# First layer's mixer: TensorE's order fixed step by step from the gates on, and one gate or output projection ahead of the first chunk

## The chip, the cores and the metric

The kernel runs on one core of one Trainium2 chip. The metric is the device time of one execution in microseconds (us). Before the change it is 2372.28 us, the median of 3 runs (2371.1 to 2372.58).

## What is computed

The reference is a trunk of two decoder layers on one sequence of 1024 tokens with 1024 features. The first layer mixes tokens with an mLSTM, a matrix memory that is carried from one chunk of 128 tokens to the next; the second uses latent attention over keys and values that are made once from the first layer's output. Each mixer is followed by an MLP. All inputs and outputs are fp32. The change concerns the first layer's mixer alone:

```python
proj = h @ w_in                               # h: normed and modulated input, 1024 x 1024
q, k, v, ig, fg, og = jnp.split(proj, ...)    # 8 heads: q, k of 64, v of 128, one input and one forget gate each
# per head and chunk of 128 tokens, with b = cumsum(log_sigmoid(f)) and m a running maximum:
log_d = b[t] - b[s] + i[s]    (s <= t)
w_intra = exp(log_d - m[t]);  w_inter = exp(b + m_prev - m[t])
num = w_inter * (q @ C) + ((q @ k.T) * w_intra) @ v
C = decay * C + (w * k).T @ v                 # state for the next chunk
h = num / max(|den|, exp(-m))
out = (rmsnorm(h) * sigmoid(og)) @ w_out
```

The product of q and k with its weights is called a score below, `og` the output gate, and the last line's product the output projection.

## The kernel before, in words

**Products.** Every fp32 matrix product is made of three TensorE products of operands split into a high and a low part (`mm3`, lines 230 to 234). A 128-row weight panel is loaded by SyncE into a `raw` buffer (4 of them) and split by `wsplit` (lines 186 to 193): ScalarE rounds it into `wh` (line 189), VectorE takes the rest into `wl` (line 190). `wh` and `wl` come from a pool of 8, so four panels are held at a time. One panel of a projection to feature-major layout feeds 24 products of 128x128 by 128x512; a panel of v does so too.

**Halves.** The 1024 tokens are treated as two halves of 512, `hfs[0]` and `hfs[1]`. For each half the mixer's work is cut into generators; each `yield` ends a step:

- `qk_in` projects q and k, 8 projections of 24 products each. For the first half this is done earlier, by `qk_pairs`.
- `gates_in` (line 662) makes 16 products for the gates (lines 678, 679), then `gates0` (line 738): a chain of small operations on 8 partitions, each dependent on the one before, almost all on VectorE (lines 743 to 787) with five on ScalarE (lines 752, 754, 775, 777, 779). Its second step transposes three results on TensorE (line 792, 12 small matmuls into one `pc` tile) and copies them (line 794). Line 779 makes the last of those three inputs.
- `v_in` (line 693) projects v token-major: 2 column halves of 4 weight panels, 24 products per panel, two steps per panel, into `pm` tiles.
- `intra0` (line 797) makes the scores for four pairs of heads: for each head a broadcast matmul into a `pc` tile (line 808) and four Exp on ScalarE (line 812); then the scores of two heads into two `ps` tiles, 64 rows each (line 820); VectorE multiplies (line 825); a last matmul (line 833) and lines 834 and 835 scale q and keep the decay. The two heads of a pair use different rows of TensorE's array (`ts(r, 64)`) and are issued alternately in the code.
- `chunks0` (line 852) goes through the four chunks of the half, three steps each: numerators (lines 869 and 876) and transposes of k (line 883, then VectorE line 885); the state's update (line 918); normalising and transposing the result (line 933).
- `og0` (line 726) is the gate projection with its three ScalarE passes (lines 731 to 733), `wout` the output projection, `split_o` (line 839) gates the chunk results and splits them for that projection (lines 845, 848, 849).

`ps`, `pc` and `pm` are PSUM pools of two tiles each. Two background generators, `bg0` and `bg1` (`bgs` for both in a row), make the adaLN vectors of later stages. A step multiplies a loaded panel on VectorE (lines 358, 360) and ends in four transposes on TensorE (line 340) and a sum (line 342); they fill gaps.

**What sets the order.** The code is written in one order, but a list scheduler at build time with its own estimate of durations reorders instructions per engine by readiness and priority. `tc.issue_after(i)` ties what is issued within it to come behind instruction `i`. Each engine executes its own list strictly in that order, waiting on semaphores where inputs or buffers are not ready. Before the change only the chunk stages (`in_turn`, line 1937) are tied: every step's TensorE work is placed behind the last TensorE instruction of the step before. In the first half `weave` mixes one step of v with 1.5 steps of scores and one of the background; in the second `weave_n` takes the rest of the q, k and v steps with 0.8 of scores each. In both, the scheduler decides what stands where.

## Time and profile before

| | |
|---|---|
| median of 3 runs | 2372.28 us |
| the profiled execution | 2374.59 us, of which 2372.9 us are the span of its instructions |
| mean granted TensorE clock | 0.995 |
| busy: TensorE (PE) | 2331.0 us (98%) |
| busy: VectorE (DVE) | 1605.9 us (68%) |
| busy: ScalarE (ACT) | 1098.1 us (46%) |
| first gate product of the first half | 81.30 us |
| first product of the first half's chunks | 149.03 us |
| first gate product of the second half | 221.12 us |
| first product of the second half's chunks | 333.75 us |

The span is counted from the first instruction to the last. A row of the timeline gives the start, the duration, engine, source line, the operation, output tile and inputs, and, in brackets, how long the engine was idle before it and which instruction's end released it. Matmuls overlap: the duration of one is longer than the distance to the next, so that distances of starts tell what each costs. An fp32 matmul (lines 792 and 820) is recorded twice, so that four of them read x8. SyncE is SP, GpSimd is POOL. Stretches of the span can be asked for with each engine's busy time and the granted clock (PEclk) in them.

### The profile page before, as it was taken

To read this page: it belongs to the slowest core of one execution; us is meant where nothing else is said; L and a number is where in the kernel's file an instruction comes from. 1 tells how busy PE (TensorE), PEld (TensorE's weight loads), DVE (VectorE), ACT (ScalarE), POOL (GpSimd) and SP (SyncE) were. 2 spreads that over 40 slices of the span, in tenths; PEclk is the share of its full clock that TensorE was granted. 3 is DMA by queue.
4 is the path that set the end of the run, shared out by engine and by line. 5 is a ranking of instruction groups with operands and counts; after the bars stand their busy time and mean duration, and the time that the engine had idled before them with its cause. 6 is when DMAs were issued, how large, how long until landed. Compare 5 with 4: busy or idle time off the path is not lost.

```text
span 2372.9 us, 31774 instructions
## 1 busy us (share of the span) xinstructions
PE 2331.0 (98%) x11797; PEld 1947.3 (82%) x11797; DVE 1605.9 (68%) x2649; ACT 1098.1 (46%) x1818; POOL 156.2 (7%) x353
## 2 busy tenths in 40 slices
PE   7999999999999999999999999999999999999998
PEld 5778778888888788888888888888888888989997
DVE  6567866877575677877773967766666478457556
ACT  4355334654343354444444544534444445655543
POOL 1000000000001110111110120001001000000000
PEclk9999999999999999999999999999999999999999
DMA  9353564545566876677753666885544552657562
GB/s 313 125 155 95 167 194 137 169 134 158 166 191 175 247 231 200 178 213 206 211 163 111 200 198 197 255 285 161 179 129 132 146 168 86 188 176 218 165 183 89
DMA packets 404252, 420.72 MB, mean 177 GB/s; under 512 B 27428, under 2 KB 301921, under 8 KB 400513
## 3 DMA queue, kind: packets, MB, share of 16 engines
q1 hardware_dynamic: 398176, 385.02, 51.6%
q0 software_dynamic: 5920, 33.66, 6.3%
q8 instruction: 93, 1.52, 0.3%
q14 instruction: 63, 0.51, 0.1%
HBM read 359.37 MB, written 92.80 MB: 191 GB/s over the span
## 4 chain that ended last, share of the span: by engine, by line
PE 85%; DVE 6%; DMA 5%; ACT 2%; issue 2%; SPq 0%; DVEq 0%; ACTq 0%
PE ps L232 14%; PE ps L233 13%; PE ps L234 13%; PE pm L232 10%; PE pm L233 10%; PE pm L234 10%; PE pc L234 2%; PE pc L233 2%; PE pc L232 2%; DMA raw<-in_a_w_in_dram 2%; DVE wl L190 1%; PE pc L1676 1%; DMA raw<-in_mlp_w_dram 1%; DMA lw<-wl 1%; ACT wh L189 1%
## 5 line engine op out<-in xcount | busy, mean ns | idle before, releaser
L190 DVE TENSOR_TENSOR wl<-raw,wh 128x1024 fp32r<-128x1024 f32 (+2 forms) x382 | 458.9, 1203 | 378.7 <-ACT wh L189 277.5
L189 ACT CAST wh<-raw 128x1024 fp32r<-128x1024 f32 (+2 forms) x382 | 394.6, 1036 | 685.6 <-PE ps L232 234.0
L232 PE MATMUL ps<-k,wl 128*128 128x512 f32 (+1 forms) x1432 | 546.3, 381 | 0.3 <-DVE tmc L746 0.2
L234 PE MATMUL ps<-k,wh 128*128 128x512 f32 (+1 forms) x1432 | 539.4, 377 | 0.0
L233 PE MATMUL ps<-k,wh 128*128 128x512 f32 (+1 forms) x1432 | 537.7, 376 | 0.0
L232 PEld LDWEIGHTS ps<-k,wl 128*128 128x128 f32 x1432 | 269.9, 189 | 52.4 <-issue 3.4
L234 PEld LDWEIGHTS ps<-k,wh 128*128 128x128 f32 x1432 | 269.6, 188 | 50.2 <-issue 0.7
L233 PEld LDWEIGHTS ps<-k,wh 128*128 128x128 f32 x1432 | 270.0, 189 | 48.9 <-issue 1.4
L198 DVE TENSOR_TENSOR k<-k,pm 128x512 f32<-128x512 f32 (+1 forms) x254 | 211.2, 859 | 84.9 <-PE pm L234 83.5
L232 PE MATMUL pm<-hd,wl 128*128 128x512 f32 x512 | 202.0, 394 | 0.5 <-ACT hd L508 0.5
L233 PE MATMUL pm<-hd,wh 128*128 128x512 f32 x512 | 200.1, 391 | 2.0 <-DVE hd L509 2.0
L234 PE MATMUL pm<-hd,wh 128*128 128x512 f32 x512 | 200.1, 391 | 0.0
L232 PE MATMUL pm<-wh,hd 128*128 128x512 f32 x488 | 192.1, 394 | 3.6 <-ACT raw L1568 3.4
L233 PE MATMUL pm<-wl,hd 128*128 128x512 f32 x488 | 190.4, 390 | 0.0
L234 PE MATMUL pm<-wh,hd 128*128 128x512 f32 x488 | 190.2, 390 | 0.0
L1568 ACT ACTIVATE raw<-pm,sm 128x128 f32<-128x128 f32 (+3 forms) x64 | 47.5, 742 | 151.8 <-DVE sm L1567 114.9
L509 DVE TENSOR_TENSOR hd<-tmp,hd 128x512 fp32r<-128x512 f32 x128 | 88.1, 689 | 40.5 <-ACT hd L508 39.9
L233 PEld LDWEIGHTS pm<-hd,wh 128*128 128x128 f32 x512 | 96.5, 188 | 22.9 <-DVE hd L509 2.8
L232 PEld LDWEIGHTS pm<-hd,wl 128*128 128x128 f32 x512 | 96.6, 189 | 21.0 <-ACT hd L508 0.9
L234 PEld LDWEIGHTS pm<-hd,wh 128*128 128x128 f32 x512 | 96.5, 189 | 20.3
L1024 POOL COPY sm<-sm 128x1 f32<-128x1 f32 x128 | 48.5, 384 | 978.9 <-DVE sm L1023 942.3
L232 PEld LDWEIGHTS pm<-wh,hd 128*128 128x128 f32 x488 | 91.7, 188 | 23.7 <-ACT raw L1568 5.5
(395 smaller groups left out, 4013.5 us busy)
## 6 DMA issues: line engine op xcount, KB each, us to landing
raw<-in_mlp_w_dram SPq DMA_DIRECT2D x240, 512.0 KB, 4.4
raw<-in_ada_w_dram SPq DMA_DIRECT2D x80, 512.0 KB, 4.4
raw<-in_a_w_in_dram SPq DMA_DIRECT2D x48, 512.0 KB, 4.5
sums<-in_mlp_w_dram POOLq DMA_DIRECT2D x96, 256.0 KB, 4.6
raw<-sums SPq DMA_DIRECT2D x64, 256.0 KB, 3.7
xs<-k SPq DMA_DIRECT2D x40, 256.0 KB, 3.6
raw<-in_kv_ada_w_dram SPq DMA_DIRECT2D x16, 512.0 KB, 4.0
raw<-in_a_w_out_dram SPq DMA_DIRECT2D x16, 512.0 KB, 4.7
```

The lines of the kernel that those rows point to most:

```text
L189: nc.scalar.copy(hi[:, :n], r[:, :n])
L190: i = nc.vector.tensor_sub(lo[:, :n], r[:, :n], hi[:, :n].bitcast(F32))
L198: return f(*a, **k)
L232: nc.tensor.matmul(o, ll, rh, start=start, stop=False, **m)
L233: nc.tensor.matmul(o, lh, rl, start=False, stop=False, **m)
L234: pe_last[0] = nc.tensor.matmul(o, lh, rh, start=False, stop=stop, **m)
L509: nc.vector.tensor_sub(lo, u, hi.bitcast(F32))
L1024: now = nc.gpsimd.tensor_copy(seen, flag)
L1568: nc.scalar.activation(pr[:, :n], f, AF.Exp, bias=m, scale=SCALE, accum_out=l)
L1676: nc.tensor.transpose(pt[:, ts(2 * e + i, P)], u.prs[i][:, ts(b + e, P)], ident)
```

## The change

`go`, which runs one step of a generator and ties its TensorE instructions behind those of the step before, moves up and is used for nearly everything from the first half's gates to the second half's chunks. `share` runs a main generator step by step and, by given rates, background and side steps between them. `some_of` gives the first n steps of a generator.

First half: the gate products; five steps of v, each with one background step; the gates' transposes; then each further v step is followed by one background step and on average 1.85 score steps, and what is left of the scores comes at the end. Second half: gate products, two q/k steps, `split_o`, two more q/k steps with two background steps each, the gates' transposes, then the remaining four q/k steps with 2 score steps and 3 background steps each, then the v steps with 0.9 and 1.7.

`in_turn` takes one step of the wide work (the gate projection in the first half, the output projection of the first half in the second) ahead of the first chunk step, and none behind that first step; its background work is tied too. 67 background steps are taken before the MLP in place of 71. The number and kind of instructions of each engine are unchanged.

```diff
--- before.py
+++ after.py
@@ -1934,34 +1934,56 @@
         ada_kv(0), ada_line(kv_cols()[2:] + ada_cols(1, SH1) + ada_cols(1, SC1))
     )
 
+    last, end = [None], object()
+
+    def go(gen):
+
+        traced = nc.cur_bb.bb.instructions
+        top = traced[-1]
+        if last[0] is None:
+            r = next(gen, end)
+        else:
+            with tc.issue_after(last[0]):
+                r = next(gen, end)
+        for i in reversed(traced):
+            if i is top:
+                break
+            if i.engine == pe_last[0].ins.engine:
+                last[0] = i
+                break
+        return r
+
     def in_turn(wide, steps, fill):
 
-        traced = nc.cur_bb.bb.instructions
-        last = [None]
-
-        def go(gen):
-            top = traced[-1]
-            if last[0] is None:
-                r = next(gen, StopIteration)
-            else:
-                with tc.issue_after(last[0]):
-                    r = next(gen, StopIteration)
-            for i in reversed(traced):
-                if i is top:
-                    break
-                if i.engine == pe_last[0].ins.engine:
-                    last[0] = i
-                    break
-            return r
-
+        go(wide)
         n = 0
-        while go(steps) is not StopIteration:
-
-            if n % 3 < 2:
+        while go(steps) is not end:
+
+            if n and n % 3 < 2:
                 go(wide)
-            next(fill, None)
+            go(fill)
             n += 1
-        drain(wide)
+        while go(wide) is not end:
+            pass
+
+    def share(main, side, bg, per, bgs_per):
+
+        a = b = 0.0
+        while go(main) is not end:
+            a, b = a + per, b + bgs_per
+            while b >= 1.0:
+                b -= 1.0
+                go(bg)
+            while a >= 1.0:
+                a -= 1.0
+                go(side)
+
+    def some_of(g, n):
+        for _ in range(n):
+            v = next(g, end)
+            if v is end:
+                return
+            yield v
 
     bgs = chain(bg0, bg1)
     drain(qk_pairs(hfs[0], w0, modulate0(hfs[0].h, xT0, 1)))
@@ -1969,23 +1991,32 @@
         nc.sync.dma_start(
             xt_d[0][2 * b * P : (2 * b + 2) * P].rearrange("(k p) n -> p k n", p=P), xT0.t[b]
         )
-    drain(with_bg(gates_in(hfs[0]), bgs, 1))
+    g0, v0 = gates_in(hfs[0]), v_in(hfs[0])
+    go(g0)
     x1 = load_x1()
-    drain(weave(with_bg(v_in(hfs[0]), bgs, 1), intra0(hfs[0]), 1.5))
+    share(some_of(v0, 5), iter(()), bgs, 0, 1.0)
+    go(g0)
+    scored = intra0(hfs[0])
+    share(v0, scored, bgs, 1.85, 1.0)
+    while go(scored) is not end:
+        pass
     y1 = rms_x1(x1)
     hfs[1].h = Split()
     n1 = norm0(hfs[1].h, x1, y1, A0, adac(0, SH1))
     in_turn(og0(hfs[0], hdv), chunks0(hfs[0]), n1)
     drain(n1)
 
-    drain(gates_in(hfs[1]))
-    main = chain(twice(qk_in(hfs[1])), v_in(hfs[1]))
-    for _ in range(4):
-        next(main)
+    g1, qk1, scored = gates_in(hfs[1]), qk_in(hfs[1]), intra0(hfs[1])
+    go(g1)
+    go(qk1)
+    go(qk1)
     drain(split_o(hfs[0]))
-    for _ in range(2):
-        next(main)
-    drain(weave_n(with_bg(main, bgs, 1.7), intra0(hfs[1]), 0.8))
+    share(some_of(qk1, 2), iter(()), bgs, 0, 2.0)
+    go(g1)
+    share(qk1, scored, bgs, 2.0, 3.0)
+    share(v_in(hfs[1]), scored, bgs, 0.9, 1.7)
+    while go(scored) is not end:
+        pass
     drain(bg0)
     B0 = gate(1, NG(0, 1), adac(0, G1))
     A1 = gain(2, NG(0, 2), adac(0, SC2))
...
-    last, end = [None], object()
-
-    def go(gen):
...
```

How the change moves instructions shows at three places. In these rows stands the source line, the operation, the output and the inputs with the program's numbers, and the shape; the lines are those of the kernel before.

First place: TensorE in the first half, around the gates' transposes (`tmc_111`, `tmc_115` and `tmc_112` are the three results of the gate chain, the last one from line 779; `pm` are v's accumulators, `wh` and `wl` v's weight panels, `k4` the input's parts). Before:

```order
L232 MATMUL pm_132_750<-wh_155_866,k4_53_293 128x512
L792 MATMUL pc_119_705<-ident_64,tmc_111_658 128x8
L233 MATMUL pm_132_750<-wl_156_867,k4_52_292 128x512
L234 MATMUL pm_132_750<-wh_155_866,k4_52_292 128x512
L232 MATMUL pm_131_749<-wh_164_923,k4_55_295 128x512
L233 MATMUL pm_131_749<-wl_165_924,k4_54_294 128x512
L234 MATMUL pm_131_749<-wh_164_923,k4_54_294 128x512
```

After:

```order
L232 MATMUL pm_126_722<-wh_140_803,k4_53_293 128x512
L233 MATMUL pm_126_722<-wl_141_804,k4_52_292 128x512
L234 MATMUL pm_126_722<-wh_140_803,k4_52_292 128x512
L792 MATMUL pc_142_819<-ident_64,tmc_111_658 128x8
L792 MATMUL pc_142_819<-ident_64,tmc_115_667 128x8
L792 MATMUL pc_142_819<-ident_64,tmc_112_659 128x8
```

Before, the first transpose stood among the products of v's third panel, the second 22 rows later inside the fourth, and the third right after three more products; 84 products of v lay between the gate products and the third one. After, all twelve stand together behind 60 products of v, in the middle of its third panel, and the next product of v stands behind them.

The chain itself, on VectorE, from the third operation on (`wl` are low parts of weight panels; `tmc` the chain's values). Before:

```order
L745 COPY tmc_112_659<-ps_110_641 8x512
L190 TENSOR_TENSOR wl_165_924<-raw_163_921,wh_164_923 128x1024
L746 COPY tmc_113_660<-ps_110_641 8x512
L747 SCALAR_TENSOR_TENSOR tmc_112_659<-tmc_113_660,cols_72,tmc_112_659 8x512
L751 SCALAR_TENSOR_TENSOR tmc_113_660<-tmc_112_659 8x512
L753 TENSOR_SCALAR tmc_114_666<-tmc_113_660 8x512
```

After:

```order
L753 TENSOR_SCALAR tmc_114_666<-tmc_113_660 8x512
L755 SCALAR_TENSOR_TENSOR tmc_113_660<-tmc_114_666,tmc_113_660 8x512
L190 TENSOR_TENSOR wl_162_929<-raw_160_926,wh_161_928 128x1024
L756 SCALAR_TENSOR_TENSOR tmc_115_667<-tmc_112_659,tmc_115_667 8x512
L757 TENSOR_TENSOR tmc_115_667<-tmc_115_667,tmc_113_660 8x512
L760 SCALAR_TENSOR_TENSOR tmc_112_659<-ones_69,tmc_115_667 8x128 x4
L763 TENSOR_TENSOR tmc_111_658<-tmc_111_658,tmc_112_659 8x512
```

Before, one panel's line 190 stood within the chain, early. After, one stands here and another some rows further on, between two of the scans of line 766: two in all. In the second half it is one before and two after; there the eight operations of line 845 (which `split_o` issues) stand ahead of the chain in both, and the four of line 849 inside it in both.

Second place: TensorE at the scores of the first half (`ps` take the scores, `pc` the broadcasts and the background's transposes). Before, from the second pair on (the first stands head by head among v's second and third panels):

```order
L340 MATMUL pc_147_842<-ident_64,tma_117_700 128x128 x4
L820 MATMUL ps_161_909<-k4_79_373,k4_81_375 128x128 x4
L833 MATMUL pc_149_851<-RM_124,selW_118 128x512
L808 MATMUL pc_153_858<-RM_124,e8_116 128x512
L820 MATMUL ps_162_910<-k4_79_373,k4_81_375 128x128 x4
L808 MATMUL pc_159_887<-RM_124,e8_116 128x512
L833 MATMUL pc_167_946<-RM_124,selW_118 128x512
L820 MATMUL ps_179_1003<-k4_80_374,k4_82_376 128x128 x4
L808 MATMUL pc_172_971<-RM_124,e8_116 128x512
```

After, at the first pair, from a product of v's fourth panel on:

```order
L234 MATMUL pm_126_722<-wh_148_856,k4_54_294 128x512
L340 MATMUL pc_150_874<-ident_64,tma_131_742 128x128 x4
L808 MATMUL pc_152_882<-RM_124,e8_116 128x512
L820 MATMUL ps_153_888<-k4_79_373,k4_81_375 128x128
L820 MATMUL ps_154_889<-k4_79_373,k4_81_375 128x128
```

Before, the four matmuls of one head stood together, and other kinds stood between the heads and the pairs. After, the two heads of a pair alternate (the last two rows here repeat three times more), and 24 or 36 products of v stand between one pair and the next. So it is with all four pairs of the first half. In the second half, pairs one and two stand head by head in both kernels; pair three alternates in both, and pair four alternated before with two interruptions and does so now with none.

Third place: TensorE in the first chunk of the first half (line 876 are the numerators, line 883 the transposes of k, line 580 and line 545 work for the second half's norm, line 918 the update of the state, `ps_247` the gate projection). Before, from the last product of that projection on:

```order
L234 MATMUL ps_247_1285<-k4_54_294,wh_245_1281 128x512
L580 MATMUL ps_250_1320<-ident_64,k4_122_727 128x128 x2
L580 MATMUL ps_250_1320<-ident_64,k4_123_728 128x128 x2
L876 MATMUL pm_227_1223<-k4_127_741,hd_169_968 128x130 x2
L876 MATMUL pm_227_1223<-k4_127_741,hd_187_1058 128x130
L876 MATMUL pm_227_1223<-v8_126_739,hd_187_1058 128x130
L545 MATMUL pc_249_1314<-ident_64,sm_216_1207 128x128 x4
L918 MATMUL pc_253_1332<-k4_127_741,tmc_229_1237 64x130 x4
```

After, from the last numerator on:

```order
L876 MATMUL pm_233_1253<-v8_121_712,hd_190_1100 128x130
L883 MATMUL pc_234_1262<-ident_64,k4_81_375 128x128 x2
L883 MATMUL pc_234_1262<-ident_64,k4_82_376 128x128 x2
L580 MATMUL ps_248_1312<-ident_64,k4_117_700 128x128
L545 MATMUL pc_247_1306<-ident_64,sm_214_1199 128x128 x4
L580 MATMUL ps_248_1312<-ident_64,k4_117_700 128x128
L580 MATMUL ps_248_1312<-ident_64,k4_118_701 128x128 x2
L918 MATMUL pc_251_1324<-k4_122_714,tmc_235_1267 64x130 x4
```

Before, the 24 products of the gate projection stood between line 883 and line 918. After, they stand ahead of the numerators, and between 883 and 918 there are only the transposes of lines 580 and 545. In the second half the output projection moves in the same way, and there line 918 follows line 883 directly.

More of the change, by code (lines that the diff above doesn't have):

```diff
@@ L2048, in some @@
         return v != "end"
-    last, end = [None], object()
-    def go(gen):
-        traced = nc.cur_bb.bb.instructions
-        top = traced[-1]
-        if last[0] is None:
-            r = next(gen, end)
-        else:
-            with tc.issue_after(last[0]):
-                r = next(gen, end)
-        for i in reversed(traced):
-            if i is top:
-                break
-            if i.engine == pe_last[0].ins.engine:
-                last[0] = i
-                break
-        return r
     def two_streams(dense, other, fill=iter(()), more=4):
```

## The prediction

> **What bounds the kernel.** The page comes first, and of it the chain of work that ended last.
>
> ```profile
> PE 85%; DVE 6%; DMA 5%; ACT 2%; issue 2%; SPq 0%; DVEq 0%; ACTq 0%
> ```
>
> TensorE is the bound. The change makes it do the same instructions in another order, so it can gain or lose only three things: time in which TensorE waits, time at a lower clock, and the small price of alternating between kinds of matmul. What TensorE waits for, from 68 to 150 us (the first half's gates, v and scores), as total, times and longest:
>
> ```profile
> PE pm L233 <- DVE wl L190: 1.3, 1, 1.3
> PE pm L876 <- DVE v L722: 1.2, 1, 1.2
> PE ps L820 <- DVE hd L825: 0.9, 2, 0.5
> PE pc L340 <- ACT tmc L812: 0.5, 1, 0.5
> ```
>
> And from 220 to 345 us, the second half's (two of 0.2 are left out):
>
> ```profile
> PE pm L869 <- DVE v L722: 2.3, 1, 2.3
> PE pc L340 <- ACT tmc L812: 1.0, 1, 1.0
> PE pm L233 <- DVE wl L190: 0.3, 1, 0.3
> ```
>
> A weight panel that comes late, scores that wait for their buffers, a chunk that waits for the last copy of v: 3.9 us and 3.6 us, so the most there is to win is small. TensorE's timeline says what surrounds them.
>
> ```profile
> 110.65 1.16 PE L820 MATMUL ps<-k,k 64*128 64x128 f32 x8
> 111.73 0.51 PE L833 MATMUL pc<-RM,selW 128*128 128x512 f32 x1
> ...
> 144.73 0.39 PE L234 MATMUL pm<-wh,k 128*128 128x512 f32 x1
> ...
> 147.45 0.39 PE L234 MATMUL pm<-wh,k 128*128 128x512 f32 x1
> 149.03 1.13 PE L876 MATMUL pm<-k,hd 128*128 128x130 f32 x8 [1.20 <-DVE v L722]
> ...
> 297.89 1.16 PE L820 MATMUL ps<-k,k 64*128 64x128 f32 x16
> 298.98 0.73 PE L232 MATMUL pm<-wh,k 128*128 128x512 f32 x2
> ```
>
> From 144.73 to 147.45 are twelve products of 128x512, 0.227 us each. To 149.03 it is 1.58, so that wait cost 1.35 us, 0.15 more than its 1.20; I add this to each. One head's four scores cost 1.08 us (110.65 to 111.73). Where the heads alternate, at 297.89, both cost 1.09: half. Last, the granted clock (the third number from the right) in stretches of 3.4 us:
>
> ```profile
> 121.60:125.00 3.40, 3.19 (x8) 2.52 (x9) 3.40 (x5) 0.66 (x1) 2.58 (x1) 0.50 0.84 273
> 824.80:828.20 3.40, 1.59 (x8) 1.00 (x7) 2.82 (x5) 1.50 (x2) 0.52 (x1) 1.00 0.98 270
> 828.20:831.60 3.40, 3.40 (x10) 2.62 (x9) 3.08 (x3) 0.50 (x1) 0.00 (x0) 0.50 1.16 430
> 329.80:333.20 3.40, 1.67 (x8) 1.05 (x6) 3.29 (x7) 0.68 (x1) 0.00 (x0) 1.00 0.82 219
> 333.20:336.60 3.40, 2.69 (x20) 2.16 (x21) 3.40 (x6) 1.96 (x4) 0.00 (x0) 1.00 0.74 213
> ```
>
> After a stretch with much idle time TensorE runs the next at half clock, which costs half of it, 1.7 us. The two slow stretches begin 706.6 us apart, 207 times 3.413. Read on that grid, 1.81 us of idle time (3.40 less 1.59, at 824.80) brought one and 1.73 (at 329.80) didn't. The one at 121.60 follows the 1.3 us for a panel, among the thin matmuls of the scores.
>
> **What the change removes.** In the first half the four kinds of wait go with the order that made them, the last because a projection now stands ahead of the chunk: 3.9 + 5 x 0.15 = 4.6 us. The slow stretch at 121.60 goes with them, 1.7. All four pairs alternate: 4 x 1.08 = 4.3. Together 10.6. In the second half 3.6 + 3 x 0.15 = 4.0 go, and the interruptions of one pair, of which no row is shown: 0.6, an estimate of about half of its 1.09. Together 4.6.
>
> **What it adds: the gates' transposes.** TensorE now reaches line 792 after a fixed number of products, whether the chain is done or not, and the rest of v or of q and k queues behind it.
>
> ```profile
> 85.12 0.69 DVE L743 COPY tmc<-ps 8x512 f32<-8x512 f32 x1 [4.49 <-PE ps L679]
> ...
> 87.22 1.20 DVE L190 TENSOR_TENSOR wl<-raw,wh 128x1024 fp32r<-128x1024 f32 x1
> ...
> 91.77 0.68 DVE L755 SCALAR_TENSOR_TENSOR tmc<-tmc,tmc 8x512 f32<-8x512 f32 x1
> ```
>
> ```profile
> 100.86 0.63 ACT L779 ACTIVATE tmc<-tmc 8x512 f32<-8x512 f32 x1 [0.31 <-DVE tmc L778]
> ...
> 248.71 0.61 ACT L779 ACTIVATE tmc<-tmc 8x512 f32<-8x512 f32 x1
> ```
>
> ```profile
> 225.35 0.39 PE L232 MATMUL ps<-k,wl 128*128 128x512 f32 x1
> ```
>
> First half: the chain is released by the gate products at 85.12 and its last value is there at 101.49, 16.4 us later, with one line 190 (1.20) inside. A second makes it 17.6. TensorE's cover is 60 products, 13.6 us: with the hand-overs of 0.1 it stands for 4.1 us. Before, the cover was 84 products and a pair of scores. Second half: TensorE goes on from the gates at 225.35, and the last value is there at 249.32, 24.0 us later; a second line 190 makes it 25.2; the cover is four projections, 96 x 0.227 = 21.8: 3.4 us.
>
> **The clock behind these waits.** Of 4.1 us at least 2.0 lie in one stretch of the 3.413 grid wherever it falls, so a slow stretch follows. Where that one overlaps the wait itself it costs less; I take 1.5. The 3.4 can be cut into 1.7 and 1.7, which by the row at 329.80 is let pass, so 0.9. The Trainium skill, "TensorE: Matmul & The Clock Gate", Part 1, has the clock fall after at least one idle window of about 3.4 us on a free-running grid, and the section "Why this matters for your kernels" warns of gaps over about 3 us only; by that the first wait would hold such a window at one position in five, the second hardly ever, and the sum below would be 2.1 us better. The trace agrees on the grid, but its clock fell after less than a whole idle window.
>
> **Buffers.** What is placed in TensorE's order by hand can stand before its buffer is free. Waits of this kind are the 0.5 and 1.0 at line 340 and the 0.9 at line 820; the upper end is a panel that is asked for late:
>
> ```profile
> raw<-in_a_w_in_dram SPq DMA_DIRECT2D x48, 512.0 KB, 4.5
> ```
>
> First half: a broadcast (line 808) whose `pc` tile is still to be read by line 834, which stands on VectorE behind a line 190 of such a panel. Between 0.5 and 4.5; I take 2.0, since a panel is asked for ahead by the buffers that it has. Second half: background transposes and scores at three places, 0.5 each, 1.5; between 0 and 3.
>
> **The chunk stages.** Before, line 918 waited once, although a projection stood ahead:
>
> ```profile
> 155.93 0.60 PE L580 MATMUL ps<-ident,k 128*128 128x128 f32 x4
> ...
> 157.26 1.05 PE L545 MATMUL pc<-ident,sm 128*128 128x128 f32 x8
> 158.25 0.66 PE L918 MATMUL pc<-k,tmc 128*64 128x130 f32 x8
> 159.41 0.55 PE L918 MATMUL pc<-k,tmc 128*64 128x130 f32 x5 [0.50 <-ACT tmp L548]
> 150.64 0.69 DVE L885 TENSOR_TENSOR tmc<-pc,gc 128x512 f32<-128x512 f32 x1 [0.29 <-PE pc L883]
> 155.67 1.05 ACT L189 CAST wh<-raw 128x1024 fp32r<-128x1024 f32 x1 [0.67 <-PE ps L232]
> ```
>
> That 0.5 goes. Now line 918 of the first chunk comes 1.6 us after line 883 (0.60 of line 580 and 0.99 of 545, from its start to the next), while line 885 may stand behind a line 190: 1.20 + 0.69 and 0.3 of hand-over, less 1.6, is 0.6. Line 580 behind the next projection needs a buffer that is freed behind a cast (1.05): 1.3, between 0.5 and 2. Fewer alternations in three chunks: 0.6 won, an estimate of 0.1 for each of six. Net 0.5 - 0.6 - 1.3 + 0.6, 0.8 lost. In the second half line 918 follows line 883 at once: 0.69 + 0.3 = 1.0 lost.
>
> **The sum.** First half 10.6 - 4.1 - 1.5 - 2.0 - 0.8 = 2.2 won. Second half 4.6 - 3.4 - 0.9 - 1.5 - 1.0 = 2.2 lost. Four background steps move behind the MLP's start: 16 transposes in a stage with waits of its own, nothing taken, 1 us either way. In all nothing, 2374.6 against the profiled 2374.59. That execution was 2.3 above the median of 2372.28, so the forecast is 2372.3: within 0.2% of before, 4.7 us, about what a measurement of this kernel can tell from no change.
>
> **Rivals.** Faster: the waits at line 792 are short. The two line 190 fall into gaps of the chain, the clock isn't lowered, and buffers are free in time. Then 2 x 1.2, 2.4 and 3.5, together 8.3 us, are won on the sum: 2364.0. For it: the waits that go stand in the trace, those that come are worked out by hand. Against: 60 products (13.6) are shorter than even the bare chain, 16.4 - 1.2 = 15.2. 0.30.
>
> Slower: a loop between the engines stretches the chain. The line 190 inside it works on a panel whose `wh` buffer is free only when v's first panel is used up on TensorE, and whose cast takes 1.05 us on ScalarE; VectorE would wait there with the chain queued behind it, and TensorE waits for the chain. In the first half v's first panel ends 24 x 0.227 = 5.4 us after the gate products, with cast and hand-overs 6.7, while VectorE gets there 91.77 + 0.68 - 85.12 - 1.20 = 6.1 after them. It decides from 0.5 us on; if casts queue too, it is 2 us in each half, and a wait of 6 us holds a second stretch that lowers the clock, another 1.7: 2378.0. For it: the margins are that thin. Against: in the second half panels are used up well ahead. 0.18.
>
> That the order isn't what the text says is excluded by its rows; that what goes and what comes cancel is the forecast, 0.52.
>
> **Range.** From the faster to the slower rival, 2364.0 to 2378.0; the bounds of the buffers (2.5 up, 1.5 down in the first half, 1.5 in the second) lie within. Over 0.2% faster 0.30, within 0.52, slower 0.18.
>
> **What would show it.** Right: a wait of about 4 and one of about 3.4 us at line 792, released by line 779, and a slow stretch behind the first; scores as x16 in 1.1 us in the first half; the first numerators near 151.5 us (149.03 less 3.0, and 24 products of the moved projection, 5.4); no wait over 2 us ahead of the second half's chunks. Wrong: no wait at line 792, or one of 6; new waits over 2 us at line 820 or 808; or a difference that arises behind 400 us.

## The result, and the profile after

The changed kernel takes 2386.23 us (median of 4 runs, 2384.61 to 2388.04) against 2371.77 us before on the same chip: a ratio of 1.0061, 95% interval 1.0044 to 1.0078, so 14.5 us slower. The forecast was 2372.3 with a range from 2364.0 to 2378.0. The profiled execution took 2386.92 us with a span of 2385.2.

TensorE is busy for no longer than before (2326.2 us, where it was 2331.0), and in the chain of work that ended last a part has moved from it to VectorE and the loads:

```profile
PE 2326.2 (98%) x11797; PEld 1944.6 (82%) x11797; DVE 1604.8 (67%) x2649; ACT 1095.6 (46%) x1818; POOL 156.2 (7%) x353
...
PE 82%; DVE 7%; DMA 7%; ACT 2%; issue 2%; SPq 0%; DVEq 0%; ACTq 0%
```

TensorE has 82% of the chain where it had 85%, DVE 7% instead of 6 and DMA 7% instead of 5.

To see where the time goes, the two traces are laid over each other at equal work: TensorE's matmuls are counted by their columns, and at each count the time of the changed kernel less that of before is taken. (Counted by starts or by ends of the matmuls, such a difference comes out up to 0.4 us otherwise.) At 80 us of before the difference is -0.1 us, at 222 us -3.9, at 365 us +6.4, at 890 us +13.4 and at 2356 us +12.3. So the first half of the mixer **won** 3.8 us, the second half **lost** 10.3, and 7.0 were lost between 365 and 890 us, where the code is the same and only the four background steps are still to be done.

The first half, as TensorE's waits between 68 and 160 us (total, times, longest):

```profile
PE pc L792 <- ACT tmc L777: 3.2, 1, 3.2
PE pc L808 <- ACT tmc L812: 2.3, 1, 2.3
PE pc L792 <- ACT tmc L779: 0.7, 1, 0.7
PE pc L808 <- DVE sm L342: 0.6, 1, 0.6
```

and from its timeline there:

```profile
96.26 0.22 PE L792 MATMUL pc<-ident,tmc 8*128 8x8 f32 x1
99.65 0.23 PE L792 MATMUL pc<-ident,tmc 8*128 8x8 f32 x1 [3.17 <-ACT tmc L777]
100.59 0.83 PE L792 MATMUL pc<-ident,tmc 8*128 8x8 f32 x10 [0.71 <-ACT tmc L779]
...
109.41 1.16 PE L820 MATMUL ps<-k,k 64*128 64x128 f32 x16
...
151.12 1.73 PE L876 MATMUL pm<-k,hd 128*128 128x130 f32 x14
```

The wait for the gates is there (3.17 + 0.71), the pairs of heads alternate (x16 in one row of 1.16 us), and the first numerators stand at 151.12, behind the moved projection.

The second half, between 215 and 365 us (the first seven of the answer):

```profile
PE ps L232 <- DVE mods L426: 3.3, 1, 3.3
PE pc L918 <- DVE tmc L885: 2.4, 1, 2.4
PE pc L792 <- ACT tmc L777: 1.6, 1, 1.6
PE pc L808 <- DVE sm L342: 1.1, 2, 0.6
PE ps L232 <- DVE hd L825: 0.9, 1, 0.9
PE pm L233 <- DVE wl L190: 0.8, 1, 0.8
PE pm L232 <- DVE k L720: 0.7, 1, 0.7
```

(A further 0.3 us at line 792 stands below these seven, so that the gates cost 1.9 us there.) The two largest are new, and neither is one of the gates. The first is the output projection that now stands ahead of the chunks. Its first panel can be followed through the queues; here are the rows of VectorE, SyncE's queue, ScalarE, VectorE and TensorE, each from that engine's timeline. In SyncE's queue `in_ada_w` and `in_kv_ada_w` are background loads, `in_a_w_in` is a panel of v and `in_a_w_out` the output projection's:

```profile
326.37 0.74 DVE L360 SCALAR_TENSOR_TENSOR tma<-raw,cond,tma 128x512 f32<-128x512 f32 x1
```

```profile
319.54 0.37 SPq L211 DMA_DIRECT2D raw<-in_a_w_in_dram  x1
321.12 5.73 SPq L353 DMA_DIRECT2D raw<-in_kv_ada_w_dram  x3
327.14 18.95 SPq L211 DMA_DIRECT2D raw<-in_a_w_out_dram  x8
```

```profile
333.31 1.04 ACT L189 CAST wh<-raw 128x1024 fp32r<-128x1024 f32 x1 [3.33 <-DMA raw<-in_a_w_out_dram]
...
346.45 1.04 ACT L189 CAST wh<-raw 128x1024 fp32r<-128x1024 f32 x1 [2.40 <-DMA raw<-in_a_w_out_dram]
```

```profile
334.38 1.23 DVE L190 TENSOR_TENSOR wl<-raw,wh 128x1024 fp32r<-128x1024 f32 x1 [2.14 <-ACT wh L189]
...
347.53 1.23 DVE L190 TENSOR_TENSOR wl<-raw,wh 128x1024 fp32r<-128x1024 f32 x1 [2.70 <-ACT wh L189]
348.67 0.68 DVE L885 TENSOR_TENSOR tmc<-pc,gc 128x512 f32<-128x512 f32 x1
```

```profile
335.75 0.47 PE L232 MATMUL ps<-k,wl 128*128 128x512 f32 x1 [3.26 <-DVE mods L426]
...
349.41 0.77 PE L918 MATMUL pc<-k,tmc 128*64 128x130 f32 x10 [2.43 <-DVE tmc L885]
```

The panel's load is issued at 327.14, right after a background multiplication (line 360, to 327.11) has freed one of the four `raw` buffers, and behind three background loads in the same queue. It lands at 333.31; the cast and line 190 end at 335.61, and TensorE goes on at 335.75. (The row names line 426, a later instruction of VectorE's; what was waited for is line 190.) The second wait is of the same kind: line 885, for which TensorE waits at line 918, stands on VectorE behind a line 190 whose panel has just come. In the kernel before, v's last panel stood behind those three loads, and one load alone ahead of the output projection's panel:

```profile
311.90 5.65 SPq L353 DMA_DIRECT2D raw<-in_kv_ada_w_dram  x3
317.85 0.37 SPq L211 DMA_DIRECT2D raw<-in_a_w_in_dram  x1
325.94 0.37 SPq L353 DMA_DIRECT2D raw<-in_kv_ada_w_dram  x1
328.26 15.40 SPq L211 DMA_DIRECT2D raw<-in_a_w_out_dram  x8
```

Behind both waits of the changed kernel the clock falls:

```profile
336.60:340.00 3.40, 3.40 (x10) 2.64 (x9) 3.37 (x6) 0.93 (x2) 0.00 (x0) 0.51 0.76 212
350.80:354.20 3.40, 3.40 (x10) 2.65 (x10) 2.74 (x13) 0.90 (x3) 0.00 (x0) 0.57 0.39 113
```

Two such stretches of 3.41 us at half clock cost 1.7 us each. With the two waits (3.3 and 2.4) that is 9.1 us, about as much as the second half lost; before, TensorE waited 2.3 us ahead of the chunks, and the granted clock was 1.00 from 222 to 365 us.

The last loss, TensorE's waits between 815 and 905 us:

```profile
PE ps L232 <- DVE wl L190: 3.2, 2, 2.5
PE pm L233 <- DVE hd L509: 2.1, 1, 2.1
```

Here too a panel is late. Before, the wait for line 509 was there (1.8 us), but none for line 190.

### The profile page after: what moved, and what is told of

It reads as the page before. It is cut to its first block, busy times and chain, and to the rows that moved or that the text cites. A ratio compares the mean times of both kernels' runs of the same rounds, so it can differ in the third digit from the quotient of the medians.

```text
span 2385.2 us, 31760 instructions
## 1 busy us (share of the span) xinstructions
PE 2326.2 (98%) x11797; PEld 1944.6 (82%) x11797; DVE 1604.8 (67%) x2649; ACT 1095.6 (46%) x1818; POOL 156.2 (7%) x353
## 4 chain that ended last, share of the span: by engine, by line
PE 82%; DVE 7%; DMA 7%; ACT 2%; issue 2%; SPq 0%; DVEq 0%; ACTq 0%
PE ps L232 13%; PE ps L233 13%; PE ps L234 13%; PE pm L232 10%; PE pm L233 10%; PE pm L234 10%; DMA raw<-in_a_w_in_dram 2%; PE pc L234 2%; PE pc L232 2%; PE pc L233 2%; DVE wl L190 2%; DMA raw<-in_mlp_w_dram 1%; ACT wh L189 1%; PE pc L1676 1%; DMA lw<-wl 1%
```

## The experiments

Theory A was that the second half's order, tied by hand, makes the loss; theory B that the waits at line 792 and the clock behind them do. The table has the changed kernel and fourteen more, with what the traces laid over each other gave. "Steps" are the background steps done by the end of the second half's v, and ahead of the MLP (63 and 71 before, 59 and 67 in the changed kernel). The stretches are those of the kernel before; plus is lost. One background chunk takes seven steps: four with a load of 512 KB each, two empty ones, and one with TensorE's transposes.

| kernel | steps | to 222 us | 222 to 365 | 365 to 890 | ratio to before (95% interval) |
|---|---|---|---|---|---|
| changed | 59, 67 | -3.8 | +10.3 | +7.0 | 1.0061 (1.0044 to 1.0078) |
| first_only | 60, 68 | -1.1 | +13.2 | +0.8 | 1.0048 (1.0031 to 1.0064) |
| second_only | 62, 70 | -0.1 | +10.8 | +2.2 | 1.0043 (1.0028 to 1.0059) |
| bg71 | 63, 71 | -4.2 | +1.3 | -2.0 | 0.9982 (0.9972 to 0.9992) |
| no_ahead2 | 59, 67 | -0.7 | +9.4 | +2.8 | 1.0042 (1.0030 to 1.0054) |
| before_bg67 | 59, 67 | -1.0 | +16.9 | +5.2 | 1.0083 (1.0068 to 1.0098) |
| first_only_71 | 63, 71 | -3.8 | +0.3 | -3.0 | 0.9976 (0.9966 to 0.9986) |
| second_only_71 | 63, 71 | -0.1 | +5.5 | -1.8 | 1.0018 (1.0007 to 1.0029) |
| bg74 | 66, 74 | -2.9 | +28.8 | -4.0 | 1.0090 (1.0073 to 1.0107) |
| bg64 | 56, 64 | -1.4 | +6.4 | +11.2 | 1.0058 (1.0045 to 1.0072) |
| gap | 56, 64 | -4.4 | -0.7 | +10.8 | 1.0035 (1.0023 to 1.0047) |
| later_gates_71 | 63, 71 | -2.5 | +1.3 | +0.4 | 0.9977 (0.9964 to 0.9991) |
| first_noahead_71 | 63, 71 | +0.1 | +7.5 | +0.3 | 1.0013 (1.0002 to 1.0024) |
| late71 | 59, 71 | -3.4 | +9.5 | -2.4 | 1.0036 (1.0024 to 1.0047) |
| gap71 | 56, 71 | -5.2 | +7.0 | +8.7 | 1.0046 (1.0033 to 1.0058) |

The stretches come from one execution each, the ratios from all runs, and that one execution isn't always a typical one: for late71 it lies 8.1 us under the kernel's median, for second_only and first_noahead_71 6.3 and 6.0 over it, for the others within 4.5. Single executions of one kernel differ: 27 runs of the kernel before on one chip went from 2368.66 to 2379.89 us. Eight of these kernels (the changed one, no_ahead2, bg71, bg74, bg64, gap, late71, gap71) have the same lines to 222 us, and that stretch gave from -0.7 to -5.2.

**The change's two halves, each alone.** first_only keeps the changed lines of the first half and puts the old ones in the place of the second half's, second_only the other way round; `in_turn_old` is the loop of the kernel before:

```diff
 # first_only: second half as before, chunks of the second half as before
-    in_turn(wout(...), chunks0(hfs[1]), iter(()))
+    in_turn_old(wout(...), chunks0(hfs[1]), iter(()))
```

> The change in the first half alone (gates, v, scores, and the gate projection ahead of the first chunk); the second half is as before. Theory A, that the loss comes from the second half, where weight panels and line 885 are late: in the first half TensorE is 3.5 to 4 us ahead of before at equal work, it keeps that, 2 us faster or more in all (2366 to 2370). Theory B, that the waits at line 792 and the slow clock behind them are the loss: no faster than before, 2372 to 2375.

> The change in the second half alone, with the output projection ahead of its first chunk; the first half is as before. Theory A: 8 to 11 us lost between 225 and 365 us of the span and some 4 to 6 more later, 2384 to 2390. Theory B: about half of the whole loss, 2376 to 2380.

Both are slower by most of what the whole change lost, 1.0048 and 1.0043 against 1.0061. second_only does what theory A says (2384.36 us, 10.8 lost in the second half). But first_only, which A had faster than before, loses 13.2 us in the second half, whose source lines are those of before; and B had looked for the loss at the waits of line 792, while first_only lost nothing to 222 us. What the two have in common with the changed kernel is that fewer background steps are done, since each half's loop takes its own number. The scheduler, though, which sets TensorE's order in first_only's second half, doesn't give it the order of before: of 552 matmuls from that half's gates to its first update of the state, background apart, 62 stand elsewhere.

**Four background steps more.**

```diff
-    share(some_of(qk1, 2), iter(()), bgs, 0, 2.0)
+    share(some_of(qk1, 2), iter(()), bgs, 0, 4.0)
```

> The changed kernel with four more background steps taken in the second half's q and k steps, so that as many as before are done ahead of the MLP. Theory C, that the 6 us lost behind 400 us come from the background steps that arrive later there: TensorE behind 400 us stays at the distance from before that it has at 400, 5 to 6 us less than the changed kernel's in all, 2379 to 2381. Rival D, that those waits and slow stretches fall where they fall whenever the program is shifted: still 4 to 6 us lost behind 400 us, 2384 to 2388.

Theory C was only about what follows 400 us. The kernel gets faster by more than that, to 2370.9 us against 2374.55: 1.3 us are lost between 222 and 365 us, where 10.3 were, and 2.0 are won after. TensorE's order is tied here and stays: but for the background's own transposes, 6 of 548 matmuls from the second half's gates to its first update of the state stand elsewhere than in the changed kernel. So the four steps are the whole loss and more. Of the waits ahead of the chunks what is left is line 918's; the one for line 190 lies at 254 us, among the q and k projections (the first and the third of the answer from 215 to 365 us):

```profile
PE ps L232 <- DVE wl L190: 3.3, 2, 2.6
PE pc L918 <- DVE tmc L885: 0.8, 1, 0.8
```

**The projection ahead of the second half's chunks taken back.**

```diff
-    in_turn(wout(...), chunks0(hfs[1]), iter(()))
+    in_turn_old(wout(...), chunks0(hfs[1]), iter(()))
```

> The changed kernel without the projection ahead of the second half's first chunk. Theory E, that the projection put ahead waits for its own panel, which is loaded behind the background's, and leaves line 918 uncovered: the waits of 3.4 and 2.65 us at 332 and 347 go with the two slow stretches behind them, and a wait of about 2.4 for the last copy of v comes back, 6 to 7 us less than the changed kernel, 2379 to 2380. Rival F, that the panels are late whatever stands first: the same 3 to 4 us are waited at the first chunk or its projection, and no more than 3 us are won.

The answer lies between the two. The waits of 3.3 and 2.4 us do go, as theory E says, but the panels are late all the same, as rival F says: 9.4 us are still lost there, now with a wait of 2.2 us at line 933, whose input (line 907) stands on VectorE behind several line 190 of late panels, and with half-clock stretches elsewhere. In all the kernel is about 4.5 us better than the changed one by the ratios, where E forecast 6 to 7 and F at most 3, and the intervals of the two overlap.

**The kernel before with four steps fewer.** This is the test for theory G, that the number of background steps sets where the loads stand, whoever orders TensorE:

```diff
-    drain(with_bg(gates_in(hfs[0]), bgs, 1))
+    drain(gates_in(hfs[0]))
-    drain(weave(with_bg(v_in(hfs[0]), bgs, 1), intra0(hfs[0]), 1.5))
+    drain(weave(with_bg(v_in(hfs[0]), bgs, 0.94), intra0(hfs[0]), 1.5))
```

> The kernel before, untouched but for four background steps fewer taken in the first half (none in the gates, 15 in v), so that 59 are done by the end of the second half's v, as in the changed kernel. Theory G, that the number of background steps decides, since it sets where the background's loads stand in SyncE's queue against the weight panels: the order by hand isn't needed for the loss, 6 to 14 us slower than before, with waits for panels ahead of the second half's chunks. Theory A, that the loss comes from TensorE's order tied by hand: within 3 us of before.

2391.54 us, 1.0083: with four steps fewer the kernel before becomes at least as slow as the changed one, and loses more than the 14 us that were forecast at most. TensorE's order by hand isn't needed for the loss. TensorE waits 2.4 us for v's last panel ahead of the chunks:

```profile
PE pm L232 <- ACT wh L189: 2.4, 1, 2.4
```

(A further wait of 3.1 us for a panel lies at 269 us. Here too the scheduler has set another order, 44 of 552 matmuls, so this run alone wouldn't tell the loads from the order; bg71 and gap, where the order is tied, do.) In the order of SyncE's queue this kernel and the changed one end v alike: panel, three background loads, the output projection's first panel. Before, and with 63 steps, it is three background loads, panel, one load, the output projection's panel.

**Each half alone, with 71 steps.**

```diff
 # first_only_71
-    share(some_of(v0, 5), iter(()), bgs, 0, 1.0)
+    share(some_of(v0, 5), iter(()), bgs, 0, 1.61)
 # second_only_71
-    share(some_of(qk1, 2), iter(()), bgs, 0, 2.0)
+    share(some_of(qk1, 2), iter(()), bgs, 0, 2.5)
```

> The change in the first half alone with three background steps more there, 71 ahead of the MLP as in the kernel before. Theory G: the 12 us that the first half alone lost go, and what stays is the first half's own gain: 2 to 4 us faster than before. Theory A: still 8 us or more slower than before.

> The change in the second half alone with one background step more there, 71 in all. Theory G: the waits of 4.1 and 2.9 us for panels go; within 3 us of before. Theory A: still 6 to 10 us slower.

The first takes 2367.82 us against 2372.64, 0.9976: three steps turn a loss of 0.5% into a gain. Its second half has TensorE's order of the kernel before, but for 4 matmuls. The second is better than with 70 steps (1.0018 against 1.0043) but not within 3 us: its 5.5 us stand against theory G's forecast.

**Seven steps more, three fewer.** With seven more the loads stand against the panels as in the changed kernel, with three fewer as with 71.

```diff
 # bg74
-    share(qk1, scored, bgs, 2.0, 3.0)
+    share(qk1, scored, bgs, 2.0, 4.76)
 # bg64
-    share(some_of(qk1, 2), iter(()), bgs, 0, 2.0)
+    share(some_of(qk1, 2), iter(()), bgs, 0, 0.5)
```

> The changed kernel with seven background steps more in the second half's q and k: 66 by the end of v. A background chunk takes seven steps, four of them loads, so the loads stand against the last panels as in the changed kernel (three of them right ahead of the output projection's first panel). Theory G1, that this place is what counts: the wait of 3 us or more ahead of the output projection is there, 2380 to 2388. Theory G2, that it counts how much background is left for later: as good as with 71 steps or better, 2368 to 2372.

> The changed kernel with three background steps fewer (56 by the end of v, 64 ahead of the MLP): the loads stand against the panels as with 71 steps, but more background is left for later. Theory G1 for the stretch to 365 us: ahead of before by 2 to 4 us there, as with 71 steps, without a wait of 3 us ahead of the output projection. Theory H for what follows, that background left over costs 4 to 6 us near 850 us where it meets the MLP's panels: that loss appears again, 2372 to 2377 in all. Were the number left over the cause of both, the loss to 365 us would be at least the changed kernel's 6 us, 2385 or more.

bg74 has the most background done and is the slowest, 28.8 us lost to 365: having done more doesn't help there, which rules out G2. (It is also worse than the changed kernel; its q and k steps have 4.76 instead of 3 background steps each, and v's first panel comes 5.6 us late behind them.) bg64 lost 6.4 us from 222 to 365, where theory G1 had a gain of 2 to 4, and in all it took 2388.35 us, which is what was expected if the number of steps left over were the cause of both losses (2385 or more). The next run, with as many steps left over, speaks against that for the stretch to 365 us. Further on bg64 lost more than forecast. Waits from 815 to 905 us in bg64:

```profile
PE ps L232 <- DVE wl L190: 5.9, 2, 4.3
PE pc L1385 <- DVE tma L1377: 5.3, 1, 5.3
```

Lines 1377 and 1385 belong to what the background goes on with after these steps, the folding of the second layer's K/V and query weights: TensorE has to wait for it.

**No background behind v's last panel.**

```diff
-    share(v_in(hfs[1]), scored, bgs, 0.9, 1.7)
+    v1 = v_in(hfs[1])
+    share(some_of(v1, 14), scored, bgs, 0.9, 1.72)
+    share(v1, scored, bgs, 0.9, 0)
```

> The changed kernel without background in the last two steps of the second half's v (56 steps by the end of v), so that no background load stands between v's last panel and the output projection's first panel in SyncE's queue; the loads further ahead stand as in the changed kernel. Theory G1: the wait of 3.4 us ahead of the output projection falls under 1 us, and with the slow stretch behind it 4 to 6 us of the loss to 365 us go, while the waits at 304 and 325 us stay. Rival: the panel is late because of the DMA engines' load, and the wait is still over 2 us.

SyncE's queue in this kernel, the cast of the output projection's first panel, and TensorE at line 918:

```profile
313.62 0.37 SPq L211 DMA_DIRECT2D raw<-in_a_w_in_dram  x1
317.54 14.22 SPq L211 DMA_DIRECT2D raw<-in_a_w_out_dram  x8
```

```profile
321.49 1.05 ACT L189 CAST wh<-raw 128x1024 fp32r<-128x1024 f32 x1 [1.76 <-DMA raw<-in_a_w_out_dram]
```

```profile
339.77 0.44 PE L918 MATMUL pc<-k,tmc 128*64 128x130 f32 x4 [0.78 <-DVE tmc L885]
```

The load is issued at 317.54 rather than 327.14, the panel lies ready 12 us earlier, there is no wait ahead of the output projection, and line 918 waits 0.78 instead of 2.43. To 365 us the kernel wins 0.7 us where the changed one lost 10.3. The wait near 304 us stays (0.6), as theory G1 has it; those near 325 us, which it left standing, are gone too. TensorE's order is that of the changed kernel but for 4 matmuls of 548. Not all of the 11 us are the loads' doing: the wait of 1.9 us at line 792 is as long as in the changed kernel, but no slow stretch followed it here: 1.7 us that the loads don't explain. The 64 steps then cost 10.8 us further on, as in bg64.

**The gates' transposes later.**

```diff
-    share(some_of(v0, 5), iter(()), bgs, 0, 1.61)
+    share(some_of(v0, 8), iter(()), bgs, 0, 1.4)
     go(g0)
     scored = intra0(hfs[0])
-    share(v0, scored, bgs, 1.85, 1.0)
+    share(v0, scored, bgs, 2.55, 1.0)
```

> The first half's change alone, with 71 background steps, and the gates' transposes behind eight steps of v rather than five, the scores spread over the remaining eight. If the wait of 5.4 us at line 792 is a cost of its own, it goes, with the slow stretch behind it: 5 to 7 us faster than with five steps, 2360 to 2363 at a before of 2372. If the time only moves into waits for the scores' buffers, no more than 2 us are won on five steps, 2366 to 2369.

TensorE's waits between 80 and 160 us, in first_only_71 and then in this kernel:

```profile
PE pc L792 <- ACT tmc L777: 4.3, 1, 4.3
PE pc L792 <- ACT tmc L779: 0.7, 1, 0.7
PE pc L808 <- DVE sm L342: 0.6, 1, 0.6
```

```profile
PE pc L808 <- DVE sm L342: 2.0, 1, 2.0
PE pc L808 <- DVE dec L835: 1.6, 1, 1.6
PE ps L232 <- DVE hd L825: 1.6, 1, 1.6
PE pm L233 <- DVE wl L190: 0.8, 1, 0.8
```

The wait of 5.0 us at line 792 goes, and 6.0 us for buffers and a panel come in its place, with the scores spread over eight steps of v where it were eleven. 0.9977 is the ratio of first_only_71 again; the time only moved.

**Without the projection ahead, in the first half.**

```diff
-    in_turn(og0(hfs[0], hdv), chunks0(hfs[0]), n1)
+    in_turn_old(og0(hfs[0], hdv), chunks0(hfs[0]), n1)
```

> The first half's order alone with 71 background steps, but the chunks as before, without a projection ahead of the first. If the projection ahead is worth its place: a wait of 1 to 2 us for the last copy of v is back ahead of the first chunk, 1 to 2 us slower than with it, 2368 to 2370. If it only moves that wait to line 580 and line 918: the same to 0.5 us.

The wait for the last copy of v is back, 2.4 us by this kernel's waits, with a stretch of 3.4 us at half clock behind it (at 150.2 us), and in the place of 3.8 us won to 222 us there is 0.1 lost: the projection ahead is worth its place in the first half. But the kernel also lost 7.5 us in the second half, where first_only_71 lost 0.3, and so it is slower by more than the 1 to 2 us forecast. The source of that half is the same in both, the order isn't: the scheduler put 53 of 552 matmuls elsewhere.

**The two losses apart.**

```diff
 # late71: the four missing steps in the second half's gate projection; gap71 likewise with seven, and with gap's edit
         next(bgs)
+        if k < 4:
+            next(bgs)
```

> The changed kernel with the four missing background steps taken later, one more in each of the first four steps of the second half's gate projection (about 370 to 400 us), so that 71 are done ahead of the MLP and nothing ahead of 365 us is different. Theory H, that what is left over costs 4 to 6 us near 850 us: no loss there, while the loss to 365 us stays (9 to 11 us behind the start of the second half); 2379 to 2382 in all, 5 us less than the changed kernel. Rival: the number must be reached ahead of 365 us, and nothing is won.

> The changed kernel without background in the last two steps of the second half's v, and with one more step in each of seven steps of the gate projection, 71 in all. Theories G1 and H together: neither the loss to 365 us nor that near 850; at equal work 4 to 6 us ahead of before from 365 us to the end, 2366 to 2370 at a before of 2372 to 2375. Theory A, that the second half's tied order costs by itself: no faster than before.

In its profiled execution late71 does what theory H says: the loss to 365 us stays (9.5 us) and near 850 nothing is lost. That execution was the fastest of seven, 8.1 us under the median. By the medians it is 8.2 us slower than before, where the changed kernel was 14.5: some 6 us less, where 5 were forecast, with intervals that overlap (1.0036 and 1.0061). gap71 does not: with seven steps in the gate projection it has new waits behind 365 us of its span, 3.7 us at line 933 for line 907 and 7.7 us for one late panel (line 190) that ends at 447 us. (The first falls on the border of two columns of the table; counted with the later one they are about +3 and +12.6 in place of +7.0 and +8.7.) So this run doesn't tell whether the second half's tied order costs by itself. What tells more is bg71 against first_only_71, which differ in that order and have 71 steps each: 1.3 against 0.3 us lost from 222 to 365, 0.9982 against 0.9976.

**All queues side by side.** In SyncE's queue seven of the fifteen kernels have two to four background loads right ahead of the output projection's first panel: changed, no_ahead2, before_bg67, bg74 and late71 three, first_only four, second_only two. They lost 9.4 to 28.8 us from 222 to 365. The other eight have one there, or none (gap, gap71), and lost at most 7.5.

## Why the prediction was wrong

**Right.** The first half in the main: 2.2 us were forecast to be won and 3.8 were; the eight executions with these lines won 0.7 to 5.2, 3.3 on average. The wait for the gates was to be 4.1 us and is 3.9 (3.17 + 0.71); a slow stretch follows it; the pairs alternate in 1.1 us; line 580 was to wait 1.3 us and waits 1.2; the first numerators were to be near 151.5 and are at 151.12. In the second half the wait at line 792 is 1.9 us, where 3.4 was forecast, and the clock fell behind it all the same.

**Right in size by luck.** The buffers were to cost 2.0 us in the first half and cost 2.9 at line 808. But the 2.3 us of them were released by line 812 on ScalarE, not by line 834 behind a late panel, and bg71, with the same lines to there, has only the 0.6.

**Wrong, the step that failed.** "Four background steps move behind the MLP's start: 16 transposes in a stage with waits of its own, nothing taken, 1 us either way." The step counted those four as TensorE's work, and too much of that: not every step ends in transposes, as the description of the kernel has it, but one in seven, four of them, so that four steps have four at most. Their loads count: eight loads in every fourteen steps share one queue and four buffers with the weight panels. Where they stand when the output projection's panel is asked for depends on the number of steps done by then. bg71 shows that these four steps make the loss in both stretches, before_bg67 that as large a loss comes without the change. That the loads right ahead of the panel are what delays it is shown by gap, and by the seven kernels against the eight. With the steps held at 71 the change is 0.18% faster than before (bg71), which is within the 0.2% of the forecast.

**Wrong, a consequence of it.** In the second half the 2.3 us ahead of the chunks were counted as won, since the projection put there "now stands ahead of the chunk". It stands there, but its panel was 3.3 us late, and line 885 stood behind the next late panel: 2.4 us at line 918, where 1.0 was forecast. The bound for this was in the text (a panel that is asked for late, 4.5 us), but it was used for one place in the first half only, and the forecast for the second half stopped at 3.

**Wrong, behind 400 us.** Nothing was taken; 7.0 us were lost to 890 us, 4.6 of them near 850. There the steps left over delay the folding of the K/V and query weights, which follows them: line 1377's last work stands at 850.4 us in the changed kernel, at 825.1 before and at 821.8 in bg71. All four kernels with 67 or 68 steps have the same wait of 2.54 us for a panel, between 858 and 867 us, the two with 64 steps one of 4.3 and one of 5.3 at line 1385; with 70 or more no wait for a panel there is over 1.5. The kernels in the table with 64 steps lose 11 us between 365 and 890, with 67 or 68 from 0.8 to 7, with 70 2.2, and those with 71 that took none of them in the gate projection between -3.0 and +0.4.

**The signs.** Two that were named for being wrong came: a new wait over 2 us at line 808, and a difference that arises behind 400 us. The wait over 2 us ahead of the second half's chunks was the third thing that wasn't to be.

**The rivals.** The slower one named a loop between VectorE and TensorE inside the gate chain. The waits at line 792 were no longer than forecast, so it wasn't that. Its second half, an instruction that waits on VectorE behind a line 190 whose panel is late, is what happened at line 885, in another place.

**Settled in part.** second_only_71, first_noahead_71 and bg64 lose 5 to 8 us between 222 and 365 us although only one load stands right ahead of the output projection's panel. In each of them two stretches there ran at half clock, 3.4 us of the loss, where the kernel before and gap had none: around a wait of 3.9 us at line 792 in second_only_71 and one of 2.7 in bg64, and behind 2.6 us for the last copy of v in first_noahead_71. In second_only_71 (the granted clock is the third number from the right):

```profile
251.30:254.70 3.40, 2.35 (x13) 2.14 (x14) 3.34 (x5) 1.26 (x3) 0.00 (x0) 0.51 0.55 164
254.70:258.10 3.40, 3.40 (x9) 2.63 (x9) 2.19 (x5) 0.06 (x1) 0.00 (x0) 0.50 0.55 151
```

So what theory B named does cost in the second half, beside the panels.

**Not settled.** bg71 has second_only_71's order of TensorE in that half (but for 4 matmuls) and as many steps, and waits 0.5 us at line 792; why the gates were late in the one and not in the other isn't shown. So the share of the second half's tied order isn't known either: alone, at 71 steps, it cost 4.0 us (second_only_71 against before), and bg71 against first_only_71 gives about 1.4.

## What to carry to other kernels

Work that fills gaps has a phase: when a change takes a different number of its steps ahead of a stage, look at the order of the load queue at the stage's first panel, before any engine's order. Hold the number of background steps fixed when an order is tied by hand, or the result measures both at once; here the tied order of the first half is worth 0.24% at 71 steps, and three steps fewer turn that into a loss of 0.5%. So the kernel to take is the change's first half with 71 steps (2367.82 us, 0.9976, interval 0.9966 to 0.9986), which later_gates_71 equals. And look at where the scheduler put things in every run: the same source lines don't mean the same order.

## What the runs showed of the hardware

Here a wait was often paid twice. In the changed kernel's mixer, the waits at line 792 in both halves (3.9 and 1.9 us) were followed by these stretches of TensorE (the granted clock is the third number from the right):

```profile
101.70:105.10 3.40, 3.40 (x10) 2.64 (x10) 0.61 (x2) 0.00 (x0) 0.00 (x0) 0.58 0.00 0
247.90:251.30 3.40, 3.40 (x10) 2.66 (x9) 0.00 (x0) 0.00 (x0) 0.00 (x0) 0.51 0.00 0
```

With the two shown further up, four of the five waits of 1.8 us and more there brought a stretch at about half clock, 1.4 to 1.7 us each by these rows; the 2.3 us at line 808 didn't. The Trainium skill, "TensorE: Matmul & The Clock Gate", Part 1, has the clock fall after an idle window of about 3.4 us. Here less was enough, and the length of a wait didn't decide: 1.9 us at line 792 brought a slow stretch in the changed kernel and none in gap, and 2.3 us at line 808 none. On the grid of 3.41 us on which the slow stretches begin, that last wait is cut in two (the number behind the comma is TensorE's busy time, so 1.2 and 1.1 us were idle):

```profile
125.10:128.50 3.40, 2.21 (x10) 1.50 (x8) 0.00 (x0) 1.02 (x2) 0.00 (x0) 1.00 0.70 181
128.50:131.90 3.40, 2.28 (x10) 1.92 (x11) 3.12 (x4) 3.05 (x10) 0.00 (x0) 1.00 0.24 53
```

Ahead of three of the slow stretches 2.4 to 2.6 us were idle (in those from 97.8, 333.3 and 346.9 us); ahead of the one at 247.9 only 1.4, less than the 1.7 that let the clock stand in the kernel before. So where a wait lies on the grid counts, but idle time alone doesn't give the border.
